# Position bias of a sliding-window attention: rows overlapped while loading instead of planes spread out in DRAM first

## The chip, the cores and the metric

The kernel runs on one core of one Trainium2 chip. The metric is the device time of one execution in microseconds (us); lower is better.

## The reference, cut to what matters

One decoder block on 256 tokens of 2048 channels, in float32. Two attentions run side by side on the same input: one with a compressed latent (16 heads) and one over a sliding window of 128 positions (32 heads of 64 channels, 4 key/value heads). Their gated sum goes through an output projection, and a ConvFFN follows. The part at issue is the bias of the sliding window:

```python
dist = BLOCK + a[:, None] - bidx[None, :]              # query a, key b of a band of 256 keys
bias = rel_bias[t5_bucket(dist)]                       # 32 buckets x 32 heads
mask = (dist >= 0) & (dist < WINDOW) & (kpos >= 0)
s = jnp.where(mask, s + bias, NEG)
```

The bias of a head depends on query and key only through their distance, so its 128 x 256 plane is one row of 383 values, shifted by one element for each query.

## The kernel before

Weights are float32 and stream from DRAM in tiles of 128 x 1024 (512 KB), all issued on the SyncE queue (SP). Each becomes two float32r parts: ScalarE (ACT) casts it (`whi`, L116), VectorE (DVE) subtracts (`wlo`, L117), and TensorE (PE) then makes three products for each block (L129 to L131). Before the ConvFFN there are five tiles each of `raw`, `whi` and `wlo`.

The first part makes the adaLN terms (`w_ada`; DVE sums their products into `acc`, L235) and the early columns of `w_in`, by groups of K chunks. The sums of these columns lie in `pair` tiles; DVE adds to most of them (L360), GpSimd (POOL) to a third (L358). In the last group, hooks after certain column pairs start other work: `toeplitz` (L303) after pair 3, `keys` (L423) after pair 9, the first heads' projections (`pair_proj`) after pair 15; norms of the latents (L384 to L402) lie between. Then come 16 attention steps, `step(h)`, each with one head of the latent attention and two of the window, with weight tiles and products of other parts between them. Output projection and ConvFFN follow.

`toeplitz` loads a one-hot table and a mask, makes the 32 rows of 384 values with one matmul, adds the mask (`ud`, L313), and writes every row 128 times, each time one element further to the left, into four DRAM tensors `skew` of 1 MB (L316, on SP). `step(h)` loads its two planes of 128 x 256 from there (`bias`, L508, issued on POOL, two buffers). `keys` scales the window's keys on POOL (`ksf`, L432), splits them (L434, L435), and the scores (L524) are taken against these. One DVE instruction for each block adds the bias and takes the row's maximum (L528).

Each engine runs its instructions in the order in which the compiler put them, which follows the program's order and a schedule worked out ahead; DMAs issued by SP or POOL stand in these orders too.

Of the kernel before, what the change touches and what calls it, by code (L numbers as in the profile page):

```python
# [23 lines left out]
KGS = [2, 2, 2, 2, 4, 4]   # K chunks of w_in taken together while the first adaLN terms stream in  # L24
SHARE = [99, 99, 99, 2, 2, 2]   # of so many tiles of these terms' weights one goes to VectorE, the others to TensorE
NEARLY = 8                 # steps whose w_in columns are produced while the adaLN terms stream in
LATS = (3, 4, 5, 6, 7, 8, 9)    # pairs of these columns after which a part of the latents is normed
HOOKS = (3, 9, 15)         # and those after which the bias table, the keys and the first heads are made
PADD = 3                   # of so many pairs one is summed on GpSimd
PUMP = 1.3                 # how far the first adaLN terms' weights run ahead  # L30
RATES = (0.5, 0.8, 0.3, 0.5)    # background tiles loaded with each weight tile, in the four parts that follow
SPREAD = 7.0               # steps of two heads over which the other w_in columns are spread
NORMS = "dpdpda"           # engines that divide the six blocks of a step's softmax (VectorE, GpSimd, ScalarE)
SCT = (2, 4)               # of five long products after the attention, those in the score banks
NW1 = (5, 5, 5)            # weight tiles (raw, high, low part) before the ConvFFN
NW2 = (4, 6, 6)            # and from then on
ORDK = 5                   # pair of chunks of the second h before which no weights of later columns are split
NBLK = 24                  # [P, 512] tiles of the attention part
WT = 1024                  # floats on a partition in one weight tile
# [4 lines left out]
def block_kernel(ctx: ExitStack, tc: tile.TileContext, a, out: bass.AP):  # L44
# [19 lines left out]
    def bank2():  # L64
        """after the attention its banks serve the long products too"""
        turn["i"] += 1
        return bank("sc" if turn["i"] % 5 in SCT else "mm")

# [1 line left out]
    bg = {"gen": [], "rate": 0.0, "due": 0.0}  # L70

    def pump(n=None):
        """Emits background loads: n of them, or as many as the rate makes due."""
        if n is None:
            bg["due"] += bg["rate"]
        else:
            bg["due"] = n
        while bg["due"] >= 1.0 and bg["gen"]:
            bg["due"] -= 1.0
            if next(bg["gen"][0], "end") == "end":  # L80
                bg["gen"].pop(0)
# [23 lines left out]
    class Weights:  # L105
        """Tiles of one weight block, split into two float32r parts."""
# [19 lines left out]
    def mm3(o, w, x, start, stop):  # L126
        """out channels on the partitions: weights stationary"""
        (wh, wl), (xh, xl) = w, x
        pe.matmul(o, wh, xh, start=start, stop=False)  # L129
        pe.matmul(o, wh, xl, start=False, stop=False)  # L130
        pe.matmul(o, wl, xh, start=False, stop=stop)  # L131

    def mm3t(o, w, x, half, start, stop):
        """tokens on the partitions: activations stationary"""
        (wh, wl), (xh, xl) = w, x
        ch, cl = xh[:, half * P:half * P + P], xl[:, half * P:half * P + P]
        pe.matmul(o, ch, wh, start=start, stop=False)  # L137
        pe.matmul(o, ch, wl, start=False, stop=False)  # L138
        pe.matmul(o, cl, wh, start=False, stop=stop)  # L139

    def turn_pe(o, x):
        """o = x transposed, moved as it is"""
        pe.transpose(o, x, ident)
# [3 lines left out]
    def split_pair(src, pl, tag, bufs, eng=dve):  # L147
        """[P, 2 T] -> two chunks, each as its two float32r parts"""
# [30 lines left out]
    # g_pre_mix | g_pre_ffn | g_post_mix | g_post_ffn | g_q_lat | g_kv_lat  # L179
# [10 lines left out]
    # silu(c), as stationary blocks padded to 32 columns  # L190
# [9 lines left out]
    # rms of x  # L200
# [11 lines left out]
    def ada_gen(src, width, rows, col, on_pe, share=10**9, spread=False):  # L212
        """One product of silu(c) with 4*width columns of w_ada; src [n, P, nj * 4 * width].
        Row 32 g of rows[:, col:col + width] gets columns g*width .. of it."""
# [35 lines left out]
    def early_gen(kg, k0, s):  # L250
        """scale and shift of K chunks k0 .. k0 + s, then these chunks of h"""
# [7 lines left out]
        # columns of the product: [scale (s*128) | shift (s*128)]  # L259
# [4 lines left out]
        # ps[:, 4 b + g] = product columns g*w + b*128 ..  # L264
# [19 lines left out]
    def cols_gen(which, dst, bofs, gofs):  # L284
        """one of the later adaLN terms as columns; times a gain (the scale: 1 + it)"""
# [5 lines left out]
        # ps[:, 4 b + g] = columns g*512 + b*128  # L291
# [9 lines left out]
    skew = [dram.tile([8, P, T], F32, name=f"skew{i}") for i in range(4)]  # L301

    def toeplitz():  # L303
# [10 lines left out]
        for kv in range(4):  # L314
            r = ud[8 * kv:8 * kv + 8, :]
            nc.sync.dma_start(skew[kv], bass.AP(tensor=r.tensor, offset=r.offset + 127, ap=[r.ap[0], [-1, P], [1, T]]))  # L316

# [1 line left out]
    # pair list: cq 0-2, ckv 3-4, ks 5, (kr | vs) 6 and 7, then 3 pairs for each two steps  # L319
# [4 lines left out]
    def early_z(kg, hooks):  # L324
        s, k0 = KGS[kg], k0s[kg]
        nblk = 2048 // (s * P)           # column blocks to one group of tiles
        order = []                       # column blocks, in the order of the host's columns
# [39 lines left out]
    for kg in range(len(KGS) - 1):  # L367
# [3 lines left out]
        with ExitStack() as order:  # L371
            if kg == 0:      # nothing that can wait goes before the first chunks of h
                order.enter_context(tc.issue_after(split_ins[1].ins))
            early_z(kg, {})
            drain()
# [6 lines left out]
    def lat(first, npair, width, gofs, res):  # L382
        """root mean square norm of a latent, then its float32r parts, a pair of chunks at a time"""
# [20 lines left out]
    def rope(x, n):  # L404
        """x [P, n T] in SBUF, in its place: two heads of 64 channels on the partitions"""
# [13 lines left out]
    # float32r parts of the shared rope key and of the sliding-window keys, twice on the partitions  # L419
# [3 lines left out]
    def keys():  # L423
# [5 lines left out]
        for kv in range(4):  # L429
            src = pairs[5][(kv % 2) * 64:(kv % 2) * 64 + 64, (kv // 2) * T:(kv // 2) * T + T]  # L430
            for i in range(2):
                pool.tensor_scalar(ksf[64 * i:64 * i + 64, kv * T:kv * T + T], src, 0.125, None, op0=ALU.mult)  # L432
# [4 lines left out]
    def stack(src, tag, w):  # L437
        """Two heads of 64 channels, one above the other -> for each a tile with its two float32r parts
        on the partitions: against [k; k] one pass of 128 gives the products of both parts."""
# [12 lines left out]
    def late_z(n):  # L452
        """pair n of the other w_in columns; three to each two steps (host order qs qs ga gb ga gb)"""
# [44 lines left out]
    def step(h):  # L498
# [9 lines left out]
        pool.dma_start(bias, skew[kv][2 * (h % 4):2 * (h % 4) + 2].rearrange("h p b -> p h b"))  # L508
# [5 lines left out]
        for i in range(3):  # L514
            sc = bank("sc")
            for c0, c1, q0, kw in ((0, P, 0, P), (P, 384, P, T)):
# [5 lines left out]
                else:  # L522
                    for j in range(2):
                        pe.matmul(sc[:, c0:c1], qss[i - 1][:, qsl], kss[:, j, kv, :kw], start=j == 0, stop=j == 1)  # L524
            bt = cmask if i == 0 else bias[:, i - 1, :]
            for j, (c0, c1, b0) in enumerate(((0, P, P), (P, 384, 0))):
                col = 2 * i + j
                dve.tensor_tensor_reduce(sm[:, i, c0:c1], sc[:, c0:c1], bt[:, b0:T], 1.0, sink6[:, h, col:col + 1],  # L528
# [85 lines left out]
    def down(src, nk, xs, col, yt, ssq_t, pl, nlast, last_w, hook=None):  # L614
        """[T, D] = xs @ w, times the gate and the post gain; sums of squares of the product"""
        for g in range(4):
            bs = [bank2() for _ in range(2)]
            nkt = nk // 4
            for kt in range(nkt):
# [6 lines left out]
                elif kt == nkt - nlast:  # L626
                    # the first tokens end before the others, so that their epilogue runs meanwhile
# [141 lines left out]
def _consts():  # L769
# [4 lines left out]
    # a channel's sine goes to its partner in the other half, with a sign  # L774
# [10 lines left out]
    for d in range(128):  # L785
        onehot[bucket[d], 255 - d] = 1.0
        negm[:, 255 - d] = 0.0
# [20 lines left out]
def _blocks(w, cols):  # L808
    """w [K, N] -> [p, kc, cols]"""
# [3 lines left out]
def _layout(i):  # L813
# [9 lines left out]
    # first scale and shift, by groups of K chunks  # L823
# [4 lines left out]
    for s in KGS:  # L828
        sc = wa[:, D + k0 * P:D + (k0 + s) * P]
        sh = wa[:, k0 * P:(k0 + s) * P]  # L830
        m = np.concatenate([sc, sh], 1)                       # [2048, s*256]
        nj = WT // (s * 256)
        w1.append(m.reshape(KC // nj, nj, P, s * 256).transpose(0, 2, 1, 3).reshape(KC // nj, P, WT))
        m = win[k0 * P:(k0 + s) * P][:, early]                # [s*128, cols]
# [12 lines left out]
    for n, j in enumerate((2, 3, 4, 5)):                      # gt1, sh2, sc2, gt2  # L847
# [45 lines left out]
```

## Time and profile before

| what | us |
|---|---|
| median of 3 runs | 1576.63 |
| lowest and highest run | 1572.74, 1581.98 |
| span of the profiled execution | 1579.2 |
| PE busy in it | 1472.8 (93%) |

The profiled execution's own time is not listed beside its span; its span lies 2.6 us above the median and inside the range of the three runs. Busy shares are means over the whole span. The strips of the page cut it in 40 slices of 39.5 us each.

### The profile page before, as it was taken

The page shows a single profiled execution, that of the slowest core. Times are in us where ns is not written, and L with a number is a line of the kernel's source. Part 1 is how long each engine was busy: PE and PEld are TensorE (multiplying, and loading weights), DVE is VectorE, ACT ScalarE, POOL GpSimd, SP SyncE. Part 2 cuts the span into 40 slices and gives each one's busy share as a digit, 9 for nine tenths or more (in the row PEclk, how much of TensorE's full clock was granted, in tenths as well). Part 3 has the DMA queues.
Part 4 walks back from the last instruction along what each step waited for, and adds up shares of the span by engine and source line. Part 5 has one row for each costly group of instructions (what it writes and reads, how often), then busy time and mean ns, then how long its engine had stood idle before and what let it go on. Part 6 is the DMA issues. An engine that isn't in the chain of part 4 may idle for free.

```text
span 1579.2 us, 27319 instructions
## 1 busy us (share of the span) xinstructions
PE 1472.8 (93%) x10914; PEld 1360.9 (86%) x10914; DVE 1047.3 (66%) x1384; ACT 755.3 (48%) x1165; POOL 291.8 (18%) x206
## 2 busy tenths in 40 slices
PE   7999998049999999999989999999999999999998
PEld 6888997038989889887879999999999999888886
DVE  3489876048878796977778778766666566444443
ACT  4544434034664465575665445544444445344342
POOL 0034212345362453432000100000000000000000
PEclk9999999579999999999989999999999999999999
DMA  9889875458968785856938878855656657666663
GB/s 372 292 314 328 302 229 138 73 160 266 318 213 288 234 297 191 282 176 231 371 138 289 271 264 276 257 178 186 184 180 184 186 181 233 198 191 190 195 190 104
DMA packets 105631, 361.28 MB, mean 229 GB/s; under 512 B 11776, under 2 KB 16320, under 8 KB 104992
## 3 DMA queue, kind: packets, MB, share of 16 engines
q1 hardware_dynamic: 104064, 355.02, 68.8%
q0 software_dynamic: 1440, 4.53, 0.9%
q8 instruction: 85, 1.39, 0.4%
q14 instruction: 42, 0.34, 0.1%
HBM read 351.11 MB, written 8.39 MB: 228 GB/s over the span
## 4 chain that ended last, share of the span: by engine, by line
PE 76%; DMA 7%; DVE 6%; issue 4%; SPq 3%; ACT 1%; POOL 1%; DVEq 0%; ACTq 0%; POOLq 0%
PE bk_mm L129 12%; PE bk_mm L131 12%; PE bk_mm L130 11%; DMA raw<-in_w_in_dram 4%; PE bk_sc L129 4%; PE bk_sc L130 4%; PE bk_sc L131 4%; PE bk_mm L137 4%; PE bk_mm L138 4%; PE bk_mm L139 4%; PE bk_sc L138 3%; PE bk_sc L139 3%; PE bk_sc L137 3%; SPq L316 3%; DVE wlo L117 2%
## 5 line engine op out<-in xcount | busy, mean ns | idle before, releaser
L117 DVE TENSOR_TENSOR wlo<-raw,whi 128x1024 fp32r<-128x1024 f32 (+3 forms) x472 | 587.9, 1252 | 389.3 <-ACT whi L116 383.4
L116 ACT CAST whi<-raw 128x1024 fp32r<-128x1024 f32 (+3 forms) x472 | 478.4, 1020 | 606.5 <-PE bk_mm L130 160.5
L129 PE MATMUL bk_mm<-h_hi,whi 128*128 128x256 f32 x1824 | 523.2, 287 | 66.4 <-ACT whi L116 65.8
L131 PE MATMUL bk_mm<-h_hi,wlo 128*128 128x256 f32 x1824 | 517.9, 285 | 3.4 <-DVE wlo L117 3.4
L130 PE MATMUL bk_mm<-h_lo,whi 128*128 128x256 f32 x1824 | 518.4, 284 | 0.1
L129 PEld LDWEIGHTS bk_mm<-h_hi,whi 128*128 128x128 f32 x1824 | 351.0, 193 | 79.9 <-ACT whi L116 67.2
L131 PEld LDWEIGHTS bk_mm<-h_hi,wlo 128*128 128x128 f32 x1824 | 350.7, 193 | 5.1 <-DVE wlo L117 4.5
L130 PEld LDWEIGHTS bk_mm<-h_lo,whi 128*128 128x128 f32 x1824 | 351.3, 193 | 1.1 <-issue 0.8
L235 DVE SCALAR_TENSOR_TENSOR acc<-raw,csil,acc 128x1024 f32<-128x1024 f32 (+1 forms) x141 | 189.4, 1343 | 44.1 <-DMA raw<-in_w_ada_dram 43.6
L129 PE MATMUL bk_sc<-h_hi,whi 128*128 128x256 f32 x560 | 159.2, 284 | 0.0
L130 PE MATMUL bk_sc<-h_lo,whi 128*128 128x256 f32 x560 | 158.9, 284 | 0.0
L131 PE MATMUL bk_sc<-h_hi,wlo 128*128 128x256 f32 x560 | 158.9, 284 | 0.0
L739 POOL TENSOR_TENSOR sa<-sa,u 128x512 f32<-128x512 f32 x22 | 31.7, 1442 | 468.7 <-DVE u L733 468.7
L129 PEld LDWEIGHTS bk_sc<-h_hi,whi 128*128 128x128 f32 x560 | 108.1, 193 | 0.4 <-issue 0.4
L130 PEld LDWEIGHTS bk_sc<-h_lo,whi 128*128 128x128 f32 x560 | 108.0, 193 | 0.0
L131 PEld LDWEIGHTS bk_sc<-h_hi,wlo 128*128 128x128 f32 x560 | 107.9, 193 | 0.0
L358 POOL TENSOR_TENSOR pair<-pair,part 128x512 f32<-128x512 f32 x35 | 65.3, 1865 | 190.2 <-ACT part L357 190.1
L137 PE MATMUL bk_sc<-whi,g_hi 128*128 128x512 f32 x176 | 68.6, 390 | 0.0
L137 PE MATMUL bk_mm<-whi,g_hi 128*128 128x512 f32 x176 | 68.6, 390 | 0.0
L138 PE MATMUL bk_mm<-wlo,g_hi 128*128 128x512 f32 x176 | 68.5, 389 | 0.0
L139 PE MATMUL bk_mm<-whi,g_lo 128*128 128x512 f32 x176 | 68.5, 389 | 0.0
L138 PE MATMUL bk_sc<-wlo,g_hi 128*128 128x512 f32 x176 | 68.5, 389 | 0.0
(201 smaller groups left out, 2100.7 us busy)
## 6 DMA issues: line engine op xcount, KB each, us to landing
raw<-in_w_ada_dram SPq DMA_DIRECT2D x192, 512.0 KB, 5.0
raw<-in_w_up_dram SPq DMA_DIRECT2D x176, 512.0 KB, 4.5
raw<-in_w_in_dram SPq DMA_DIRECT2D x116, 512.0 KB, 5.5
raw<-in_w_down_dram SPq DMA_DIRECT2D x88, 512.0 KB, 4.4
raw<-in_w_o_dram SPq DMA_DIRECT2D x32, 512.0 KB, 4.8
raw<-in_w_uqn_dram SPq DMA_DIRECT2D x16, 384.0 KB, 4.2
skew<-ud SPq DMA_DIRECT2D x4, 1024.0 KB
bias<-skew POOLq DMA_DIRECT2D x16, 256.0 KB, 4.7
```

What stands on the lines that cost most here:

```text
L116: act.copy(hi[:, :n], raw[:, :n])
L117: dve.tensor_tensor(lo[:, :n], raw[:, :n], hi[:, :n].bitcast(F32), op=ALU.subtract)
L129: pe.matmul(o, wh, xh, start=start, stop=False)
L130: pe.matmul(o, wh, xl, start=False, stop=False)
L131: pe.matmul(o, wl, xh, start=False, stop=stop)
L137: pe.matmul(o, ch, wh, start=start, stop=False)
L138: pe.matmul(o, ch, wl, start=False, stop=False)
L139: pe.matmul(o, cl, wh, start=False, stop=stop)
L235: dve.scalar_tensor_tensor(acc[:, :w], r, csil[:, j:j + 1], acc[:, :w], op0=ALU.mult, op1=ALU.add)
L316: nc.sync.dma_start(skew[kv], bass.AP(tensor=r.tensor, offset=r.offset + 127, ap=[r.ap[0], [-1, P], [1, T]]))
L358: pool.tensor_tensor(pairs[i][:, :wd], pairs[i][:, :wd], part[:, :wd], op=ALU.add)
L739: pool.tensor_tensor(sa, sa, us[1], op=ALU.mult)
```

## The change

- `toeplitz` stores the 32 rows once, in a DRAM tensor `trow` of 32 x 384 (48 KB), with one DMA issued on POOL. The four DMAs into `skew` on SP are gone.
- `step(h)` loads its two planes with one DMA whose source rows overlap: partition p reads 256 values starting at element p of a row. It is issued on POOL as before.
- For this to be possible with a rising address, the rows of the table stand in order of rising distance (`onehot` and `negm`, made on the host), so that the bias of a query comes with the keys in descending order. `keys` therefore writes the scaled keys from the last to the first (negative step in the output of L432), and the DVE instruction that adds the bias writes its result with a negative step, so that `sm` is in ascending order again. Slices of the keys, of `cmask` and of the bias are moved accordingly.

The diff also drops comments and docstrings, which are left out here.

```diff
-    skew = [dram.tile([8, P, T], F32, name=f"skew{i}") for i in range(4)]
+    trow = dram.tile([32, USTR], F32, name="trow")
+    def down_order(x):
+        return bass.AP(tensor=x.tensor, offset=x.offset + x.ap[-1][1] - 1, ap=[*x.ap[:-1], [-1, x.ap[-1][1]]])
...
         dve.tensor_tensor(ud, negm, psu[0:32, :USTR], op=ALU.add)
-        for kv in range(4):
-            r = ud[8 * kv:8 * kv + 8, :]
-            nc.sync.dma_start(skew[kv], bass.AP(tensor=r.tensor, offset=r.offset + 127, ap=[r.ap[0], [-1, P], [1, T]]))
+        pool.dma_start(trow, ud)
...
-                pool.tensor_scalar(ksf[64 * i:64 * i + 64, kv * T:kv * T + T], src, 0.125, None, op0=ALU.mult)
+                pool.tensor_scalar(down_order(ksf[64 * i:64 * i + 64, kv * T:kv * T + T]), src, 0.125, None, op0=ALU.mult)
...
-        pool.dma_start(bias, skew[kv][2 * (h % 4):2 * (h % 4) + 2].rearrange("h p b -> p h b"))
+        r = trow[2 * h:2 * h + 2, :]
+        pool.dma_start(bias, bass.AP(tensor=r.tensor, offset=r.offset, ap=[[1, P], [USTR, 2], [1, T]]))
...
-                        pe.matmul(sc[:, c0:c1], qss[i - 1][:, qsl], kss[:, j, kv, :kw], start=j == 0, stop=j == 1)
-            bt = cmask if i == 0 else bias[:, i - 1, :]
-            for j, (c0, c1, b0) in enumerate(((0, P, P), (P, 384, 0))):
+                        pe.matmul(sc[:, c0:c1], qss[i - 1][:, qsl], kss[:, j, kv, T - kw:], start=j == 0, stop=j == 1)
+            for j, (c0, c1) in enumerate(((0, P), (P, 384))):
                 col = 2 * i + j
-                dve.tensor_tensor_reduce(sm[:, i, c0:c1], sc[:, c0:c1], bt[:, b0:T], 1.0, sink6[:, h, col:col + 1],
+                bt = cmask[:, P - c0:T] if i == 0 else bias[:, i - 1, :c1 - c0]
+                to = sm[:, i, c0:c1]
+                dve.tensor_tensor_reduce(to if i == 0 else down_order(to), sc[:, c0:c1], bt, 1.0, sink6[:, h, col:col + 1],
...
-        onehot[bucket[d], 255 - d] = 1.0
-        negm[:, 255 - d] = 0.0
+        onehot[bucket[d], 127 + d] = 1.0
+        negm[:, 127 + d] = 0.0
```

## Rows read from the trace of the kernel before

**Rows 1.** The page's strips over the whole span, 40 slices of 39.5 us: busy tenths of PE, the granted TensorE clock in tenths, GB/s of the DMAs.

```profile
PE   7999998049999999999989999999999999999998
PEclk9999999579999999999989999999999999999999
GB/s 372 292 314 328 302 229 138 73 160 266 318 213 288 234 297 191 282 176 231 371 138 289 271 264 276 257 178 186 184 180 184 186 181 233 198 191 190 195 190 104
```

**Rows 2.** Waits from 250 to 345 us, longest first: who waited for whom, us in total, times, longest.

```profile
DVE wlo L117 <- ACT whi L116: 72.3, 2, 71.7
ACT whi L116 <- DMA raw<-in_w_in_dram: 68.0, 1, 68.0
...
PE bk_mm L129 <- ACT whi L116: 65.8, 1, 65.8
POOL blk_lo L152 <- DMA skew<-ud: 42.9, 1, 42.9
POOL bias L508 <- issue: 24.1, 1, 24.1
```

**Rows 3.** The SP queue's instructions in order of time (start, us, engine, line, what): the four `skew` writes and what stands on both sides of them.

```profile
245.17 2.66 SPq L95 DMA_DIRECT2D raw<-in_w_in_dram  x2
249.73 0.33 SPq L95 DMA_DIRECT2D raw<-in_w_ada_dram  x1
250.19 50.09 SPq L316 DMA_DIRECT2D skew<-ud  x4
300.32 23.94 SPq L95 DMA_DIRECT2D raw<-in_w_in_dram  x2
```

**Rows 4.** The chain that ended last, in the same stretch (start, us, what).

```profile
279.09 21.19 SPq L316
300.32 33.90 DMA raw<-in_w_in_dram
334.30 1.04 ACT whi L116
```

**Rows 5.** PE's instructions in order of time at the two ends of its stall; in brackets, the idle time before one and what ended it.

```profile
269.36 0.28 PE L131 MATMUL bk_mm<-h_hi,wlo 128*128 128x256 f32 x1
335.40 0.58 PE L129 MATMUL bk_mm<-h_hi,whi 128*128 128x256 f32 x1 [65.76 <-ACT whi L116]
...
336.66 0.58 PE L131 MATMUL bk_mm<-h_hi,wlo 128*128 128x256 f32 x1 [0.47 <-DVE wlo L117]
337.04 0.41 PE L129 MATMUL bk_mm<-h_hi,whi 128*128 128x256 f32 x1
...
339.46 0.29 PE L130 MATMUL bk_mm<-h_lo,whi 128*128 128x256 f32 x1
```

**Rows 6.** Busy time of the engines by stretches: us, then PE, PEld, DVE, ACT, POOL busy (instructions), granted clock, DMA share, GB/s.

```profile
220.00:240.00 20.00, 20.00 (x169) 20.00 (x169) 15.88 (x20) 10.59 (x14) 4.53 (x2) 1.00 0.78 253
250.00:380.00 130.00, 58.15 (x448) 55.55 (x447) 54.94 (x51) 36.13 (x51) 50.59 (x36) 0.75 0.56 135
270.00:335.00 65.00, 0.00 (x0) 0.00 (x0) 0.00 (x0) 0.70 (x1) 15.76 (x16) 0.53 0.49 96
335.00:380.00 45.00, 39.14 (x291) 36.95 (x292) 42.15 (x34) 26.60 (x39) 33.98 (x19) 0.95 0.69 216
399.00:718.00 319.00, 308.17 (x2359) 286.35 (x2358) 259.23 (x488) 184.89 (x418) 136.27 (x100) 0.99 0.73 245
```

**Rows 7.** DVE's instructions in order of time before the stall: three of the four splits of weight tiles after 250 us.

```profile
250.09 1.84 DVE L117 TENSOR_TENSOR wlo<-raw,whi 128x1024 fp32r<-128x1024 f32 x1
...
256.30 1.22 DVE L117 TENSOR_TENSOR wlo<-raw,whi 128x1024 fp32r<-128x1024 f32 x1
...
261.28 1.21 DVE L117 TENSOR_TENSOR wlo<-raw,whi 128x1024 fp32r<-128x1024 f32 x1
```

**Rows 8.** The page's DMA issues: what, engine, count, KB each, median us from issue to landing.

```profile
raw<-in_w_in_dram SPq DMA_DIRECT2D x116, 512.0 KB, 5.5
...
out_dram<-y SPq DMA_DIRECT2D x8, 256.0 KB, 2.2
...
oh<-in_onehot_dram SPq DMA_DIRECT2D x1, 48.0 KB, 4.5
```

**Rows 9.** DMAs from 250 to 340 us: the planes of the first two steps, issued while the `skew` writes ran (median us to landing at the end).

```profile
bias<-skew POOLq DMA_DIRECT2D x2, 256.0 KB, 17.1
```

**Rows 10.** POOL's instructions in order of time during the stall.

```profile
274.95 1.47 POOL L508 DMA_DIRECT2D bias<-skew  x2 [24.10 <-issue]
276.46 7.25 POOL L432 TENSOR_SCALAR ksf<-pair 64x256 f32<-64x256 f32 x8
```

**Rows 11.** DMAs from 400 to 720 us, the attention steps: POOL's queue (packets, MB, share of 16 engines) and the loads of the planes.

```profile
q0 software_dynamic: 1120, 3.67, 3.7%
...
bias<-skew POOLq DMA_DIRECT2D x14, 256.0 KB, 4.4
```

**Rows 12.** The load of the planes of the last step but one (POOL) and the first DVE instruction that reads them.

```profile
684.80 0.76 POOL L508 DMA_DIRECT2D bias<-skew  x1 [6.91 <-DVE mx L528]
...
703.33 0.34 DVE L528 CUSTOM_DVE_ANT_0 sm<-bk_sc,bias,c_sink 128x128 f32<-128x128 f32 x1
```

**Rows 13.** The DVE instructions that add the bias, and those that add the latent attention's mask, with their shapes: ns min/median/max.

```profile
L528 DVE CUSTOM_DVE_ANT_0 sm<-bk_sc,bias,c_sink x64: 332/410/484, 399.3 to 717.0; 128x128 f32<-128x128 f32 x32, 128x256 f32<-128x256 f32 x32
L528 DVE CUSTOM_DVE_ANT_0 sm<-bk_sc,c_cmask,c_sink x32: 339/412/483, 398.6 to 709.8; 128x128 f32<-128x128 f32 x16, 128x256 f32<-128x256 f32 x16
```

## Prediction, made before the changed kernel was run

> **What bounds the kernel now.** I read the page's strips first [rows 1]. PE is busy nine tenths or more nearly everywhere; the one deep hole is in the seventh to ninth slice (237 to 355 us), where PE falls to 8, 0 and 4 tenths, the granted clock to 5 and 7 tenths, and the DMAs move 138, 73 and 160 GB/s where the slices around them move 229 to 328. So the question is what makes this hole, not what bounds the kernel on average. The list of waits in that stretch answers it from the bottom up [rows 2]: PE waits 65.8 us for a cast weight tile, ACT waits 68.0 us for a raw tile of `w_in`, DVE 71.7 us for the cast. The SP queue in order of time shows why the tile is late [rows 3]: it issued weight tiles every few us until 249.73, then the four `skew` writes held it for 50.09 us, and the next two tiles' issue took another 23.94 us. The chain that ended last runs through the same places [rows 4]: SP at L316 until 300.3, then 33.90 us from the issue of that tile to its landing, where the median for such a tile is 5.5 us [rows 8]. The 4 MB of `skew` in flight explain the late landing: the hole ends only when these bytes are through.
>
> Outside the hole PE sets the pace: just before it, it is busy 20.00 of 20 us with DVE at 15.88 [rows 6]. So I take it that a microsecond of stall removed here ends the kernel a microsecond earlier, as long as another engine doesn't use it up before 400 us.
>
> **The change, part by part.**
>
> *The four writes on SP go.* The next weight tile can then be issued at 250.2 instead of 300.3, or at 251.9 if it needs the raw tile that the split then running sets free [rows 7]. With the median landing it arrives at 251.9 + 5.5 = 257.4, and cast and split follow in some 2.3 us (1.04 for the cast [rows 4], 1.22 for the split [rows 7]). PE had tiles in hand until 269.4 [rows 5], so this tile would be ready at 259.7, 10 us ahead of need. The stall of 65.8 us is gone as a whole, not only the 50 us of SP's.
>
> *The clock.* While PE stood, the granted clock was 0.53 of full, that is the lower level (1.2 GHz) nearly throughout [rows 6]. After the stall the matmuls start 0.21 us apart instead of 0.12, until about 339.5 [rows 5]. From 335.4 to 337.7 PE started six products; at 0.12 they take 0.72 us, and 0.47 was a wait, so 2.3 - 0.5 - 0.7 = 1.1 us went to the clock, and some 0.8 more by 339.5, estimated from the same spacing. I take 1.9 us.
>
> Together 65.8 + 1.9 = 67.7 us.
>
> *What can be given back.* During the stall POOL worked 15.76 us, and PE and DVE not at all [rows 6]. POOL ran ahead there, with the planes' loads, the scaling of the keys (7.25 us) and more [rows 10]; without the stall this work lies beside PE's. Take 250 to 380 us, 130 us long [rows 6]: PE worked 58.15, DVE 54.94, POOL 50.59. After a saving of 67.7 the stretch lasts 62.3. All three fit, PE with 4 us to spare, DVE with 7, POOL with 12. PE's own work caps the saving at 130 - 58.2 = 71.8, and with the clock's 1.9 at about 74. The floor: if none of POOL's 15.76 us and none of the new wait below could be overlapped, 20 us would come back and the saving be 47. It is nearer the upper end, because PE has 10 us in hand as the stretch begins, and the two pull in opposite directions. I take 0.7 us as given back, a rounding, and 67 us as the saving.
>
> *The new write and its wait.* POOL now writes 48 KB, and the first planes' load must wait for it. No such write is in the trace; the nearest rows are the 256 KB stores of the result at 2.2 us, a load of 48 KB at 4.5 us [rows 8], and, for a DMA in the thick of the `skew` writes, 17.1 us [rows 9]. I take 4.5, since size and place are the nearest. Behind it on POOL stand the planes' loads, the keys and every third pair sum. POOL waited 24.1 us there before [rows 2], and then 42.9 us more for `skew`, because the buffer of `ud` was held until these writes were read; both shrink. So this wait costs nothing beyond the 20 us floor above, where it is counted.
>
> *The planes' loads.* Their number, size, destination and run length (1 KB) are unchanged; only the source is new, 128 overlapping rows in 3 KB of DRAM, most of them starting off any round address. That is not in the trace. Bounds: nothing, if a packet costs what it does now; and, if it costs more, what the cover allows. The load of the last step but one is issued at 684.80 and first read at 703.33 [rows 12], 18.5 us later; it lands in 4.4 [rows 11]. So the landing may be four times as long before a step waits. In DMA time, the 14 loads of the steps take 3.7% of 320 us, 11.8 us, in a stretch with the DMAs 0.73 busy [rows 6, 11]; at twice the cost the share becomes 0.77, and nothing waits. I take nothing.
>
> The Trainium skill ("DMA: Bandwidth & Descriptors", How a descriptor splits into AXI transactions) speaks against it: a run that doesn't start on a 256-byte boundary costs one more transaction and fetches bytes that aren't used. By its figures an average row here would take about 36 beats instead of 32, an estimate of an eighth more, 1.5 us of DMA time over the steps; no run here shows it yet, and the sum stays as it is.
>
> *Negative steps.* Eight POOL instructions (7.25 us in all [rows 10]) and 64 DVE instructions write backwards. The trace has no negative step in a compute instruction; `c_cmask` and `bias` forms, both forward, cost the same (412 and 410 ns median) [rows 13]. The lower bound is nothing; a gain is excluded, since no element is saved. The upper: half the rate, 64 x 0.41 = 26.2 us of DVE in steps where DVE is busy 259 of 319 us and PE 308 [rows 6]; DVE would reach 285, still under PE, so perhaps 10 of them would show. I take nothing, as the instruction is paid by elements and their number is the same.
>
> *Matmuls, mask and host tables*: same shapes in other places, no cost.
>
> **The sum.** Span 1579.2 - 67 = 1512. The runs' median is 2.6 us under the span, so 1576.6 - 67 = 1509.6; I forecast 1510 us.
>
> **Rivals.**
>
> A. POOL, or the order of instructions on it, becomes the bound between 250 and 330 us. For it: 50.6 us of POOL work and 4.5 of waiting would have to fit in 62 us, in strict order, with waits for ACT and DVE between. Against: POOL's products there are mostly needed later. It gives back 7 to 20 us: 1517 to 1530.
>
> B. Backward writes run at half rate: about 10 us back, 1520, up to 26, 1536.
>
> C. The loads from overlapping rows are slow, because all 16 DMA engines read the same 3 KB. This is the rival on the other side. It decides through the weight stream, which shares these engines: the steps last 319 us with the DMAs 0.73 busy, of which 0.04 is the planes. To lose all 67 us, the 14 loads would have to fill 319 + 67 - 0.69 x 319 = 166 us of DMA time instead of 11.8, 14 times as much; then the kernel is where it was, and above that slower, as at 20 times, 236 us: about 1580 to 1650. At 8 times it costs nothing by this sum, but late planes would (35 us to land against 18.5): some 5 to 15 us for the tightest steps. Nothing in the trace speaks for a factor so large; nothing reads one spot like this either.
>
> D. The stall is removed but a second limit lies right under it, so that the change does less than it says: the norms and rotations of the latents follow in 340 to 380 us, where DVE is busy 42.2 of 45 us after the stall [rows 6]. The DVE sum above (54.9 of 62) leaves room; at worst 1520 to 1530.
>
> **Chances.** Forecast (1500 to 1517): 0.70. A and D: 0.16. B: 0.07. C: 0.07, of which 0.03 ends slower than before, 0.01 level, and the rest in between. Half a per cent, 8 us, is about what a measurement of this kernel can tell from no change; the three runs before spread over 9 us. So faster 0.96, same 0.01, slower 0.03. The range: low end, the cap of 74 us and 2 us of spread, 1500; high end, A and B without their tails, 1527.
>
> **What would show it.** Right: no instruction between weight tiles on SP longer than a few us around 250; PE without a hole and the clock at full in the seventh and eighth slice; the first step's score instructions at about 330 instead of 399; bytes written in DRAM down by 4.2 MB; the planes landing in under 10 us; the bias instructions at 0.41 us. Wrong: a POOL wait of more than 10 us for the 48 KB write with PE waiting behind it (A), the bias instructions near 0.8 us (B), planes landing after 20 us or more with the weight tiles late beside them (C), DVE at its limit from 260 to 310 with PE waiting for `wlo` (D).

## The result, and the profile after

The changed kernel takes 1521.03 us (median of four runs, 1519.90 to 1523.21) against 1575.86 for the kernel before on the same chip: a ratio of 0.9651, 95% interval 0.9622 to 0.9680, or 55 us less (50 to 60). Forecast were 1510 us, with a range of 1500 to 1527. The profiled execution took 1520.17 us for a span of 1518.3, so 1.9 us lie around the span.

The page's strips of the changed kernel, 40 slices of 38 us each, to be held against [rows 1]:

```profile
PE   7999999799999999999899999999999999999998
PEclk9999999999999999999999999999999999999999
GB/s 371 295 313 328 308 234 262 178 264 306 175 306 240 298 197 274 197 208 358 183 250 259 254 277 266 225 181 183 182 181 190 182 181 242 191 193 192 194 193 99
...
HBM read 351.11 MB, written 4.24 MB: 234 GB/s over the span
```

The hole of slices seven to nine is gone. One slice there, the eighth, still has PE at 7 tenths. DRAM writes are down to 4.24 MB.

The SP queue in the place of [rows 3] (start, us, engine, line, what):

```profile
243.56 2.66 SPq L95 DMA_DIRECT2D raw<-in_w_in_dram  x2
248.13 0.33 SPq L95 DMA_DIRECT2D raw<-in_w_ada_dram  x1
249.73 4.70 SPq L95 DMA_DIRECT2D raw<-in_w_in_dram  x2
```

The next weight tile leaves at 249.73, where it left at 300.32 before. The loads of the planes, their DVE instructions and the landing of the loads (ns min/median/max; then us):

```profile
L535 DVE CUSTOM_DVE_ANT_0 sm<-bk_sc,bias,c_sink x64: 336/412/481, 337.7 to 655.1; 128x128 f32<-128x128 f32 x32, 128x256 f32<-128x256 f32 x32
...
DMA to landing us min/median/max: 3.7/5.2/7.5
```

412 ns against 410 in [rows 13]: writing backwards costs DVE nothing. The planes land in 5.2 us, 7.5 at most.

Where the time went is one stretch. Nearly the same work, from 240 us to the first scores, by windows (us; PE, PEld, DVE, ACT, POOL busy; granted clock, DMA share, GB/s), first of the kernel before, then of the changed one:

```profile
240.00:400.00 160.00, 86.89 (x673) 82.23 (x672) 81.26 (x79) 50.23 (x72) 61.81 (x41) 0.80 0.61 160
```

```profile
240.00:339.00 99.00, 87.15 (x676) 83.80 (x675) 86.10 (x81) 51.15 (x73) 65.16 (x43) 0.97 0.70 221
```

160 us became 99: the difference of the two spans (60.9) lies here. PE's idle time fell from 73.1 to 11.9. And two columns rose: DVE is busy 4.8 us more and POOL 3.4 us more. Part of that is two more instructions of each in the window; cut at the same work, from the start of `ud` to the first DVE instruction that adds the bias, DVE is busy 71.84 us before (71 instructions) and 76.84 after (70), POOL 56.05 and 58.82. The windows inside the stretch show where PE's remaining loss lies:

```profile
260.00:280.00 20.00, 19.64 (x159) 19.14 (x157) 18.95 (x14) 14.07 (x17) 19.50 (x11) 1.00 0.73 220
280.00:290.00 10.00, 4.53 (x29) 3.91 (x28) 10.00 (x10) 3.02 (x5) 9.53 (x7) 0.91 0.23 56
290.00:300.00 10.00, 8.94 (x68) 8.74 (x67) 6.52 (x7) 5.37 (x9) 5.79 (x7) 0.92 0.67 227
```

From 280 to 290 PE works 4.53 of 10 us while DVE is full and POOL nearly. PE's instruction that ends the gap, and what DVE and POOL did at that time (start, us; idle before in brackets):

```profile
288.61 0.58 PE L131 MATMUL bk_mm<-blk_hi,wlo 128*128 128x256 f32 x1 [4.29 <-DVE wlo L117]
```

```profile
281.96 5.73 DVE L406 SCALAR_TENSOR_TENSOR pair<-pair,c_gcol,rl 128x256 f32<-128x256 f32 x4
287.61 2.34 DVE L117 TENSOR_TENSOR wlo<-raw,whi 128x768 fp32r<-128x768 f32 x2
```

```profile
280.86 2.32 POOL L152 TENSOR_TENSOR blk_lo<-pair,blk_hi 128x512 fp32r<-128x512 f32 x1
283.14 2.86 POOL L363 TENSOR_TENSOR pair<-pair,part 128x512 f32<-128x512 f32 x2
285.97 1.44 POOL L152 TENSOR_TENSOR blk_lo<-pair,blk_hi 128x512 fp32r<-128x512 f32 x1
```

Four norm instructions of the latents (L406) take 5.73 us, 1.43 each, and the split that PE waits for stands behind them. In the kernel before, six of the same instructions took 2.46 us, 0.41 each, while POOL was idle. In the changed kernel the same six took 2.88 us, 0.48 each, beside POOL's scalings of the keys, which read one tensor; the slow four lie beside POOL instructions that read two:

```profile
257.43 2.46 DVE L401 SCALAR_TENSOR_TENSOR pair<-pair,c_gcol,rl 128x256 f32<-128x256 f32 x6
```

```profile
255.72 2.88 DVE L406 SCALAR_TENSOR_TENSOR pair<-pair,c_gcol,rl 128x256 f32<-128x256 f32 x6
```

### The profile page after: what moved, and what is told of

It reads as the page before. It is cut to its first block, busy times and chain, and to the rows that moved or that the text cites. A ratio compares the mean times of both kernels' runs of the same rounds, so it can differ in the third digit from the quotient of the medians.

```text
span 1518.3 us, 27322 instructions
## 1 busy us (share of the span) xinstructions
PE 1472.3 (97%) x10914; PEld 1361.0 (90%) x10914; DVE 1050.1 (69%) x1384; ACT 754.4 (50%) x1165; POOL 286.9 (19%) x207
## 3 DMA queue, kind: packets, MB, share of 16 engines
HBM read 351.11 MB, written 4.24 MB: 234 GB/s over the span
## 4 chain that ended last, share of the span: by engine, by line
PE 79%; DVE 9%; DMA 7%; issue 3%; ACT 1%; POOL 0%; DVEq 0%; SPq 0%; ACTq 0%; POOLq 0%
PE bk_mm L129 12%; PE bk_mm L131 12%; PE bk_mm L130 12%; PE bk_mm L137 4%; PE bk_mm L138 4%; PE bk_mm L139 4%; DMA raw<-in_w_ada_dram 4%; PE bk_sc L130 4%; PE bk_sc L129 4%; PE bk_sc L131 4%; PE bk_sc L138 3%; PE bk_sc L137 3%; PE bk_sc L139 3%; DVE wlo L117 3%; DVE acc L235 3%
```

## The experiments

Two questions were open: whether the bytes written or something else in the change brought the gain, and what took back the part of 67 us that is missing. The theory for the second: POOL's work, which had been done during the stall, now lies beside DVE's, and the two slow each other. Rivals: the negative steps, the overlapping rows, the write on POOL, and ScalarE's order of work.

**The kernel before, profiled again** (`e0_before`, no edit).

> The kernel before, unchanged, for a second profile of it. The changed kernel's profiled span is 60.9 us shorter, but its median time only 54.8 us. If the length of the stall at the four writes differs from execution to execution, and the first profile caught a long one, this profile has a span 3 to 8 us shorter than 1579.2, SP's four writes and the first tile's landing are shorter by the same, and PE's idle time in the stall is 58 to 63 us instead of 65.8. If the stall is as long every time, its idle time is within 1 us of 65.8 and the span differs from 1579.2 for another reason.

It took 1579.43 us (1572.07 to 1585.34; the kernel before beside it 1578.69), with a span of 1577.5. Its longest waits in the stall:

```profile
PE bk_mm L129 <- ACT whi L116: 65.5, 1, 65.5
```

The stall is as long as in the first profile (65.8), and the first expectation was wrong for these two executions. The runs of the kernel before differ by up to 13 us; both profiles are of executions near the median or above it, so whether the stall is shorter in the short ones (1572 to 1574) isn't shown. The run also shows the 1.9 us around the span.

**A sixteenth of the bytes** (`e1_small_skew`; `s` stands for the step's two heads of `skew`, whose rows the loads now read overlapped; the values of the bias are left out).

```diff
-    skew = [dram.tile([8, P, T], F32, ...
+    skew = [dram.tile([8, 8, T], F32, ...
-            ... ap=[r.ap[0], [-1, P], [1, T]]))
+            ... ap=[r.ap[0], [-1, 8], [1, T]]))
-        pool.dma_start(bias, skew[kv][...].rearrange("h p b -> p h b"))
+        pool.dma_start(bias, bass.AP(tensor=s.tensor, offset=s.offset, ap=[[8, P], [8 * T, 2], [1, T]]))
```

> The kernel before, with a sixteenth of the bytes written: the four writes stay on SP, 64 KB each, and the planes are loaded from these (the bias itself is left out, its values are not the reference's). Nothing is written backwards and POOL writes nothing. The theory that the bytes were the stall expects it gone: no SP instruction over 5 us around 250, PE without a hole of more than 10 us, 1510 to 1526 us. If the loss that is left in the changed kernel at 280 to 290 us comes from POOL's and DVE's work lying beside each other, it is here too, 1517 to 1526. If it comes from the write on POOL or from backward writes, it isn't, 1508 to 1515. If the change's gain came from anything but the bytes (the queue alone, say), the time stays above 1550.

1519.88 us, ratio 0.9632 (0.9607 to 0.9658). SP's four writes and the window of the remaining loss:

```profile
247.53 2.99 SPq L316 DMA_DIRECT2D skew<-ud  x4
```

```profile
280.00:300.00 20.00, 14.74 (x98) 14.13 (x99) 16.30 (x16) 8.79 (x14) 15.31 (x13) 0.83 0.46 143
```

The whole gain is there with four writes still on SP, forward steps and no write on POOL: the stall came from what the writes carry, not from their number. Their bytes and their 1 KB rows were cut together, so this run doesn't tell the two apart. And the loss at 280 to 300 us is there too, so neither negative steps nor the write on POOL make it.

**The four full writes on POOL** (`e10_skew_on_pool`).

```diff
-            nc.sync.dma_start(skew[kv], ...
+            pool.dma_start(skew[kv], ...
```

> The kernel before, all 4 MB still written as planes, but the four writes issued on POOL instead of SP. If SP's queue, held for 50 us, is the whole stall, weight tiles go on and the time falls to 1520 to 1530 us, with POOL's descriptors late instead. If the bytes on the shared DMA engines are the other half of it, weight tiles land late all the same (15 us or more from issue to landing, 5.5 now), PE loses 20 to 50 us between 260 and 340, and the time is 1540 to 1575. If POOL, held by its own writes, blocks the pair sums, PE stops for these and the time is 1570 us or more.

1539.95 us, ratio 0.9755 (0.9736 to 0.9773), 38 us less than the kernel before and 17 more than the changed kernel, both measured beside it (1577.75 and 1522.78). DMAs from 250 to 330 us:

```profile
skew<-ud POOLq DMA_DIRECT2D x4, 1024.0 KB, 39.6
...
raw<-in_w_in_dram SPq DMA_DIRECT2D x6, 512.0 KB, 17.9
```

So the writes' place on SP's queue is the larger part of the stall: with that queue free, PE worked 10 to 13 of every 20 us from 260 to 320, and lost 26 us from 260 to 340, as the second expectation has it. The other 17 us come from two things that this run doesn't separate. Weight tiles still took 17.9 us to land instead of 5.5, while 4 MB went through the same engines, and POOL, which stood 20.6 us between its writes and the planes' loads, was late with sums:

```profile
POOL bias L508 <- issue: 20.6, 1, 20.6
PE bk_mm L129 <- ACT whi L116: 11.9, 2, 6.1
PE bk_tp L392 <- POOL tot L390: 5.5, 1, 5.5
```

Moving the writes to POOL's queue brings two thirds of the gain; not writing them brings the rest. The same writes also load the DMA engines differently from there. From 280 to 300 us the engines are 0.44 busy in the kernel before and 0.98 here (last column but one):

```profile
280.00:300.00 20.00, 0.00 (x0) 0.00 (x0) 0.00 (x0) 0.00 (x0) 9.67 (x10) 0.50 0.44 67
```

```profile
280.00:300.00 20.00, 10.07 (x58) 9.30 (x57) 9.58 (x10) 6.80 (x9) 12.42 (x11) 0.76 0.98 159
```

So in the kernel before the tiles came late with more than half of the engines' time unused; what held the transfers at 67 GB/s there, no run shows.

**Only forward steps** (`e3_forward`; it leaves out the placement of the bias).

```diff
-                pool.tensor_scalar(down_order(ksf[...]), src, ...
+                pool.tensor_scalar(ksf[...], src, ...
-                dve.tensor_tensor_reduce(to if i == 0 else down_order(to), ...
+                dve.tensor_tensor_reduce(to, ...
```

> The changed kernel with every compute instruction writing forwards; the bias then meets the wrong keys (its placement is left out). The theory of POOL and DVE slowing each other expects no change: within 3 us of 1521, the eight scalings of the keys on POOL at about 1.2 us each as now (9.56 us for all), the bias instructions at 0.41. The rival, that the negative step slows POOL, expects 0.85 to 0.91 us each as before (7.25 for all) and 1515 to 1518 us.

1519.61 us, ratio 0.9625 (0.9593 to 0.9656). The key scaling, here and in the changed kernel:

```profile
253.66 10.04 POOL L437 TENSOR_SCALAR ksf<-pair 64x256 f32<-64x256 f32 x8
```

```profile
254.90 9.56 POOL L437 TENSOR_SCALAR ksf<-pair 64x256 f32<-64x256 f32 x8
```

Forward it takes 10.04 us, backward 9.56: the rise over the 7.25 of [rows 10] has nothing to do with the step. Then DVE stood still; here it doesn't.

**Planes from separate rows** (`e4_apart`; zeros in place of the bias).

```diff
-        pool.dma_start(bias, bass.AP(tensor=r.tensor, offset=r.offset, ap=[[1, P], [USTR, 2], [1, T]]))
+        pool.dma_start(bias, a["cw_planes"][h].rearrange("h p b -> p h b"))
```

> The changed kernel with its planes loaded from a plain input of 128 separate rows for each head (zeros: the bias is left out), so that no source rows overlap; the 48 KB write stays. Mechanism of overlapping rows dear: landing falls from 5.2 us to 4.4 or less, POOL's queue from 1.2% of 16 engines to 0.9%, and the time by 4 us or more, to 1517 or less. Otherwise the share may fall but the time stays within 3 us of 1521, since the loads are issued long ahead of their use.

1519.50 us, ratio 0.9631 (0.9600 to 0.9663). The landing is 5.0 us in the median instead of 5.2, and POOL's queue takes 1.0% of the DMA engines instead of 1.2%; the time is the same. Overlap costs some 3 us of DMA time over the whole kernel (0.2% of 1518, from shares rounded to a tenth of a per cent), and none on the path.

**ScalarE's order** (`e7_tanh_late`).

```diff
-        act.activation(tg, tg, AF.Tanh, scale=0.5)
+        with tc.issue_after(vt_copy.ins):
+            act.activation(tg, tg, AF.Tanh, scale=0.5)
```

> The changed kernel with the tanh of a step's gates held behind the values' copy of its own pair of heads, so that ScalarE doesn't wait for gate columns (9.3 us on DVE, 5.3 us on POOL) with weight casts queued behind. If ScalarE's order is the cause of PE's loss at 280 to 290 us, the casts come in time, PE idles 3 to 5 us less there and the time is 1512 to 1518 us. If DVE's slow norms are, the cast is early but the split still waits for DVE, and the time stays at 1518 to 1524.

1518.70 us, ratio 0.9643 (0.9617 to 0.9669). DVE's norms and PE's wait are as they were:

```profile
282.67 5.72 DVE L406 SCALAR_TENSOR_TENSOR pair<-pair,c_gcol,rl 128x256 f32<-128x256 f32 x4
```

```profile
PE bk_mm L131 <- DVE wlo L117: 4.3, 1, 4.3
```

The edit did its work: ScalarE's waits for gate columns, 10.9 us from 260 to 320, are gone. In their place it waits 10.5 us for the norms. So these waits were real, but beside the path.

**The keys' scaling on DVE** (`e6_keys_on_dve`).

```diff
-                pool.tensor_scalar(down_order(ksf[...
+                dve.tensor_scalar(down_order(ksf[...
```

> The changed kernel with the eight scalings of the keys on DVE instead of POOL (9.56 us of POOL's unbroken work from 253 to 292). If PE's loss at 280 to 290 us comes from POOL's backlog lying beside DVE's norms of the latents, POOL's later work comes 8 to 10 us earlier, the four norm instructions (1.43 us each beside POOL, 0.41 without) run faster, PE idles 2 to 5 us less between 280 and 300, and the time is 1513 to 1519 us. If the loss comes from ScalarE's order alone, it stays: 1519 to 1524.

1520.35 us, ratio 0.9639 (0.9612 to 0.9666): not what I expected. The stretch and the norms:

```profile
260.00:280.00 20.00, 15.50 (x111) 14.64 (x110) 19.88 (x22) 12.16 (x16) 14.21 (x7) 0.91 0.49 139
280.00:290.00 10.00, 9.89 (x83) 9.68 (x82) 10.00 (x13) 3.81 (x6) 6.35 (x4) 1.00 0.68 224
```

```profile
281.80 1.66 DVE L406 SCALAR_TENSOR_TENSOR pair<-pair,c_gcol,rl 128x256 f32<-128x256 f32 x4
```

The norms are back to 0.41 us each and the loss at 280 is gone, as the theory has it. But it reappears one window earlier, where DVE is full. The keys are only 2.40 us of that. POOL, without them, began its instructions with two inputs at 255.53 instead of 264.54, and the first split beside these took three times its usual 1.22 us:

```profile
255.62 3.54 DVE L117 TENSOR_TENSOR wlo<-raw,whi 128x1024 fp32r<-128x1024 f32 x1
```

Relieving POOL by loading DVE moves the loss.

**The latents' low parts on DVE** (`e8_latsplit_dve`, and again as `e12_latsplit_again` beside the changed kernel, `e11_after`).

```diff
-            res += split_pair(pr, blkp, "blk", NBLK, pool)
+            res += split_pair(pr, blkp, "blk", NBLK, dve)
```

> The changed kernel with the low parts of the latents made on DVE (five instructions of 128x512) instead of POOL. If POOL's two-input instructions slow DVE's two-input ones beside them, the norms fall from 1.43 to under 0.7 us each, the low parts take some 0.6 us each on DVE, and the time is 1515 to 1520 us. If the 1.43 us of the norms have another cause, they stay above 1 us, DVE has 3 us more to do, and the time is 1521 to 1526.

> The changed kernel again, beside the next one on the same chip: 1517 to 1524 us, PE idle 8 to 9 us from 280 to 320, norms of the latents at 1.43 us each.

> The changed kernel with the latents' low parts on DVE, again: 1511 to 1518 us, 4 to 9 us under the changed kernel in the same call, norms at 0.41 us each. If the gap to the changed kernel was a difference of chips, the two are within 2 us here.

1514.59 us, ratio 0.9610 (0.9584 to 0.9636). The second time 1514.77, ratio 0.9599 (0.9580 to 0.9618), against 1522.78, ratio 0.9646 (0.9631 to 0.9660), for the changed kernel beside it: 8 us less. This version beats both kernels. The norms of the first time, and POOL's instruction that ends its idle time beside them:

```profile
285.47 1.66 DVE L406 SCALAR_TENSOR_TENSOR pair<-pair,c_gcol,rl 128x256 f32<-128x256 f32 x4
```

```profile
287.26 5.39 POOL L419 TENSOR_TENSOR ropet<-pair,c_sinT 32x256 f32<-32x256 f32 x3 [5.75 <-issue]
```

DVE got five instructions more, and the norms fell from 5.73 to 1.66 us, with POOL idle beside them. PE still idles in places there (5.2 us from 260 to 280), 3.4 of it for one pair sum that stands behind an adaLN sum and a low part on DVE.

How much of the 8 us this is, the profiled executions show when they are cut at the same work (us; the first two columns are the starts of `ud` and of the first DVE instruction that adds the bias):

| kernel | `ud` | first bias | between | from there to the end |
|---|---|---|---|---|
| before | 249.6 | 399.3 | 149.7 | 1179.9 |
| before, again | 247.7 | 397.9 | 150.2 | 1179.6 |
| changed | 248.0 | 337.7 | 89.7 | 1180.6 |
| changed, again | 247.6 | 337.7 | 90.1 | 1180.5 |
| low parts on DVE | 248.8 | 335.3 | 86.5 | 1176.5 |
| low parts on DVE, again | 248.8 | 336.6 | 87.8 | 1180.8 |

Between the two marks the low parts on DVE bring 2 to 4 us. The rest lies outside. There single executions differ by as much without it: `e4_apart` and `e3_forward` have the same median (1519.50 and 1519.61), but their profiled executions took 1515.12 and 1522.57 us, with 1178.5 and 1184.0 in the last column. And the two profiled executions of the second time lie only 0.8 us apart (1519.20 and 1520.02), with the norms at 1.66 and 5.73 us. So the 8 us between the medians stand as measured, but the stretch in which the norms lie accounts for less than half of them.

**Both on DVE** (`e9_keys_latsplit_dve`).

> Both: the keys' scaling and the latents' low parts on DVE. If POOL's backlog is the cause, POOL is idle for at least 15 us more of 253 to 300, the norms take 0.4 to 0.7 us each, PE idles under 3 us between 280 and 300, and the time is 1510 to 1517 us. If not, DVE is the bound with 6 us more work, and the time is 1521 to 1528.

1514.47 us, ratio 0.9606 (0.9581 to 0.9632): the same as the latents' part alone. POOL is busy 23.5 instead of 41.1 us from 253 to 300, and the norms take 0.68 us each, as expected. But DVE is 19.87 of 20 us busy from 260 to 280 and PE 14.63; the keys gave nothing more in the time.

## Why the prediction was right, and what it sized wrongly

**The stall.** Right in place and size. The first tile leaves SP at 249.73 (forecast 250.2), PE has no hole, and the idle time of 65.8 us is gone. That the late landing behind the four writes belonged to the stall, not only SP's 50 us, the rows of the kernel before say: after SP's hold alone, with the usual 5.5 us of landing and 1.0 for the cast, the stall would have ended at about 307, after 38 us (an estimate from [rows 3, 4, 5, 8]). The run with the writes on POOL, where tiles still landed late, saved 38 us too. It doesn't separate the rest from POOL's own delay.

**The clock.** The 1.9 us didn't appear. The granted clock also falls after the new gap, to 0.91 and 0.92 from 280 to 300, so some of that stretch is at the lower level again: from 289.2 to 291.8 the products start 0.21 us apart. PE's busy time between the two marks of the table was 76.7 and 78.3 us in the profiles of the kernel before and is 78.0 in both of the changed one; in the whole kernel it is 1472.3 against 1472.8.

**What is given back.** This term was mis-sized: 0.7 us, where PE's idle time outside the stall rose by 4.5 us between the two marks, from 7.2 to 11.7. With the clock's 1.9 this is most of what the forecast lacks: the stretch became 60.0 us shorter, and the span 60.9, instead of 67. I had taken POOL's 15.76 us and DVE's 54.94 from the trace as they stood and found that both fit beside PE's work. But POOL's had been done while DVE stood still, and much of DVE's while POOL did. The price of an instruction changes when the other engine works: a norm takes 0.41 us alone and 1.43 beside POOL, and a low part on POOL took 1.26 us in the stall of the kernel before, against up to 2.32 beside DVE now:

```profile
286.23 1.26 POOL L152 TENSOR_TENSOR blk_lo<-pair,blk_hi 128x512 fp32r<-128x512 f32 x1
```

What came is rivals A and D, which I had priced apart at up to 20 us and given 0.16 together, as one mechanism at a small price: POOL works without a gap from 253.4 to 287.4, DVE is at its limit, and PE waits 4.29 us for a split behind slow norms, the sign that the prediction named for D. The 1521 us lie above the 1500 to 1517 to which it gave 0.70. That DVE was close to its limit stood in the trace already: after the stall of the kernel before, PE waited 5.8 us in eight pieces for splits. Taking the low parts off POOL makes the stretch 2 to 4 us shorter. How much of this is the contention itself and how much the order, which the compiler works out anew for every edit, these runs don't separate. That the norms' price goes with POOL's neighbouring work they show: 1.43 us each beside its instructions with two inputs (six profiles), 0.48 beside its scalings, 0.41 with POOL idle (four profiles).

The Trainium skill has the rule that I should have weighed ("GPSIMD Engine Reference", Specifications): GpSimd's SBUF interfaces are shared with VectorE, with contention against DVE instructions that read two SBUF inputs. The trace agrees: the norms read two, while a pair sum, which reads one of its two from PSUM, takes 0.67 us in the middle of POOL's unbroken work, as in its idle time:

```profile
272.12 0.67 DVE L365 TENSOR_TENSOR pair<-pair,bk_mm 128x512 f32<-128x512 f32 x1
```

**The rest of the distance**, from 60.9 us between profiles to 55 between medians, is hardly more than the interval of the latter (50 to 60). The first profile's span lies on the long side of that kernel's runs, which spread from 1571 to 1585 us; with 1.9 us around it its time would be 1581, 4.5 us above the median from which I subtracted. In the profiles the stretch itself is steady (149.7 and 150.2 us before, 89.7 and 90.1 after), and the parts ahead of it and behind it vary. What varies there wasn't found, and no short execution of the kernel before was profiled.

**The new write and the planes.** Right at nothing on the path: the 48 KB landed 4.0 us after their issue, and the planes' load left 4.6 us after it (248.86 to 253.42), where I took 4.5. POOL stood idle for 2.6 us of that. Overlapping rows changed the landing by 0.2 us and the time not at all (rival C falls). **Negative steps** cost nothing on DVE (412 against 410 ns) or POOL (9.56 us against 10.04 forward), so rival B falls as well.

## What to carry to other kernels

A transfer that sits in the middle of the weight stream cost twice here, by holding its queue and by making tiles land late; ask first whether overlapping rows can be read instead of planes written. When a stall goes away, the work that other engines did inside it comes back beside the rest, and at contended prices: take durations from a stretch where both engines worked. Giving the slowed engine some of the work of the one that slows it was 2 to 4 us faster here than sharing it, although it had more to do. And cut profiles at the same work before giving a difference of medians to one cause: more than half of the 8 us lay elsewhere.

## What the runs showed of the hardware that was not expected

- DVE instructions with two SBUF inputs ran up to 3.5 times as long beside POOL's with two inputs (0.41 to 1.43 us for 128x256), but only 0.48 us beside POOL's with one; POOL's 128x512 instructions with two inputs rose from 1.26 to 2.3 us.
- The same 4 MB written in the middle of the stream delayed weight tiles to 17.9 us from issue to landing, instead of 5.5, even with SP's queue free. Written from SP, they left the DMA engines 0.44 busy; from POOL, 0.98.
- A negative step in a compute instruction's output cost nothing, on DVE or on POOL.
